# Sample attention of a streaming encoder layer in plain FP32 products, with earlier loads and later memory stores

## The chip, the cores and the metric

The kernel runs on one core of a Trainium2 chip. The core has a matrix engine (TensorE, PE; its weight loads are shown apart as PEld), VectorE (DVE), ScalarE (ACT), GpSimd (POOL) and SyncE (SP), whose queue issues nearly all DMA transfers of this kernel. Products land in PSUM, everything else lives in SBUF or in DRAM. The metric is the device time of one execution in microseconds (us); several executions are timed, and the median is compared.

## The reference

One layer of a hybrid encoder for two request groups that share the weights: a prompt of 1024 rows and a sample of 64 rows with cached keys and values. Per group: RMSNorm and a combined projection, chunk-band attention A (8 heads of 64), forgetting attention B (8 heads of 64), the output product w_o, a memory cross-attention and a convolutional FFN. The part that the change touches is the attention of the sample group; here it is, cut:

```python
def attend(q, k, v, bias, mask):
    scale = q.shape[-1] ** -0.5
    logits = jnp.einsum('bqhd,bkhd->bhqk', q, k).astype(jnp.float32) * scale
    ...
    p = jax.nn.softmax(logits, axis=-1)
    return jnp.einsum('bhqk,bkhd->bqhd', p.astype(v.dtype), v)

def chunk_band_attn_sample(qa, ka, va, cache_k, cache_v, table):   # A: 512 cached rows + 64
    k = jnp.concatenate([cache_k, ka], axis=1)
    v = jnp.concatenate([cache_v, va], axis=1)
    ...
    return attend(qa, k, v, bias, None).reshape(b, s, h * d)

def forget_attn_sample(qb, kb, vb, logf, cache_k, cache_v, cache_logf):   # B: 1024 cached rows + 64
    k = jnp.concatenate([cache_k, kb], axis=1)
    v = jnp.concatenate([cache_v, vb], axis=1)
    cum_h = jnp.cumsum(all_logf, axis=1).transpose(0, 2, 1)
    bias = cum_h[..., p:, None] - cum_h[..., None, :]
    ...
    return attend(qb, k, v, bias, mask).reshape(b, s, h * d)

def mem_kv(mem, g_mem, w_mkv, g_mk):
    kv = rms_norm(mem, g_mem) @ w_mkv
    k = rms_norm(kv[..., :D_MODEL].reshape(b, n, H_M, HEAD_DIM_M), g_mk)
    v = kv[..., D_MODEL:].reshape(b, n, H_M, HEAD_DIM_M)
```

The memory keys and values are outputs too, beside the new keys and values of both groups.

## The kernel before

**Split products.** Nearly every product of the kernel is made of two-part operands. An FP32 tensor x is split into hi, a copy of x in the type FP32R, and lo = x - hi, also FP32R; a product is then the sum of hi x hi, hi x lo and lo x hi (`SPLIT`), or of two of these where one side needs no second part. The split costs a cast on ACT and a subtraction on DVE or POOL per operand. Only transposes and a few products with a matrix of ones use plain FP32.

**Stages.** For each of eight head pairs (0 to 3 are A, 4 to 7 are B) the projection of the prompt, its norms and its attention run interleaved; the sample's rows of the same pair are projected in `proj_sample`, which stores their queries and keys to the DRAM tensor `sqk` and their values to `sv`. After the last pair the pool of projection weights is closed and a small pool `mp` is opened in its place. Now the memory projection runs: 16 units (8 blocks of 256 columns by 2 row tiles), each in four pieces of six products (`mem_piece`, L637), 65 entries in the list `line`. `mem_end` (L703) normalises and stores the finished block, `mem_turn` (L733) transposes a key block and stores it. The first 23 entries run beside the last four steps of the prompt's attention (`LEFT`), the other 42 beside the sample pairs (`PER`), in the order B, B, B, B, A, A, A, A (`SAMPLES`). A weight block of the memory projection is loaded in two halves by `load_wm` (L621) up to two units ahead and split by `split_wm` (L629, L630) one unit ahead.

**A sample pair.** `load` (L752) fetches the pair's queries and keys (sqd), new values (svn), the bias (s, one of four buffers in the pool wk), two cached key tiles of 128 partitions (kraw; the keys of one head stand in the array twice, one copy below the other) and the value chunks (vraw). `prep` (L775) splits the new values, transposes queries and keys on TensorE and splits them with the gains in `gained` (L276, L277). `splitk` (L796) and `splitv` (L806) split cached keys and values. `score` (L814) makes, per head, the products of q with hi and lo keys, adds the bias and takes the row minimum on DVE (L828, L830), and runs the exponential on ACT (L836). `turn` (L840) transposes the probabilities on TensorE and splits them (L851, L852), `sum` (L855) multiplies them with both parts of the values (L863) and joins the parts (L870, L871), `out` (L873) transposes the result.

**Order.** The loop over x runs `score` of pair x, turns and sums of pair x - 1 and `prep` and the key splits of pair x + 1, woven into the pieces of the memory projection; `load` of pair x + 1 is called at the start of step x. The first pair is loaded and prepared after the pool of the local attention (`wa`) is closed, since its tiles live in the pool `mq` that takes its place. The framework assigns buffers and writes each engine's instructions in an order of its own from priorities, dependences and modelled readiness, so an instruction may stand before others that precede it in the code; on each engine and on SP's queue the order is then fixed, and an instruction that waits holds those behind it. In the step in which the line of pieces has run out, `open_left` (L986) closes the left pools, opens those of the w_o product, and issues the loads of the mixes (after the last pair's last load, `issue_after`) and of w_o.

Of the kernel before, what the change touches and what calls it, by code (L numbers as in the profile page):

```python
# [41 lines left out]
def hybrid_step(ctx: ExitStack, tc: tile.TileContext, i: dict, o: dict):  # L42
# [658 lines left out]
    kvs, stores = {}, []  # L701

    def mem_end(n, t):  # L703
        pj = mpj.pop((n, t))[:, :256]
        if n == 7:
            kv = wk.tile([P, 256], F32, name="sq", bufs=2)
        else:
            kv = mp.tile([P, 256], F32, name="kv", bufs=2)
# [3 lines left out]
        if n < 4:  # L712
# [7 lines left out]
            nc.sync.dma_start(o["mk"][rows_, cols], kv)  # L720
        else:
# [6 lines left out]
            if n == 7:  # L728
                stores.append(store)
            else:  # L730
                store()

    def mem_turn(n, t):  # L733
        kv = kvs.pop((n, t))
        if n < 4:
            tq = bank("PT").rearrange("p (a b) -> p a b", a=4)
            for c in range(2):
                pe.transpose(tq[:, c], kv[:, c * P:(c + 1) * P], ident)
            kt = mp.tile([P, 2, P], F32, name="kt", bufs=2)
            dve.tensor_copy(kt, tq[:, 0:2])  # L740
            nc.sync.dma_start(kmd[n].rearrange("d p t -> p d t")[:, :, t * P:(t + 1) * P], kt)

    class Sample:
# [8 lines left out]
        def load(self):  # L752
            p, n = self.p, self.ctx + S
            self.qd = mq.tile([S, 4, P], F32, name="sqd", bufs=2)
            nc.sync.dma_start(self.qd.rearrange("t h d -> t (h d)"), sqk[p])
            self.vraw = mq.tile([S, 2, 64], F32, name="svn", bufs=2)
            nc.sync.dma_start(self.vraw.rearrange("t h d -> t (h d)"), sv[p])
# [7 lines left out]
            self.kraw, self.craw, self.kc, self.vc = [], [], {}, []  # L765
            for h in range(2):
                raw = mq.tile([P, T], F32, name="kraw", bufs=3)[:, :self.ctx]
                nc.sync.dma_start(raw, self.ck[2 * (p % 4) + h])
                self.kraw.append(raw)
            for c in range(self.nc):  # L770
                raw = mq.tile([P, 4, 2, 64], F32, name="vraw", bufs=3)
                self.loaded = nc.sync.dma_start(raw.rearrange("p k h d -> p (k h d)"), self.cv[p % 4, c])
                self.craw.append(raw)

        def prep(self):  # L775
            p = self.p
            self.vn = mq.tile([S, 2, 2, 64], F32R, name="svh", bufs=2)
            dve.tensor_copy(self.vn[:, :, 0], self.vraw)
            pool.tensor_tensor(self.vn[:, :, 1], self.vraw, f32(self.vn[:, :, 0]), op=ALU.subtract)
            tq = bank("tq").rearrange("p (a b) -> p a b", a=4)  # L780
            for x in range(4):
                pe.transpose(tq[:, x, :S], self.qd[:, x], ident[:S, :S])
            self.z = zq[SAMPLES.index(p) % 2]
            self.q = self.z[:, 0:4:3]
            self.kn = [mq.tile([P, 2, S], F32R, name=f"skn{x}", bufs=2) for x in range(2)]
            gained((self.q, self.z[64:, 0:4:3], tq[:, 0:2, :S], gd[:, p // 4, 0:1], LOWER),
                   (self.kn[0], self.kn[1], tq[:, 2:4, :S], gd[:, p // 4, 1:2], ALL))
# [8 lines left out]
        def splitk(self, h):  # L796
            k = self.kraw.pop(0)
            for c in range(self.nc):
                raw = k[:, c * 512:(c + 1) * 512]
                hi = mq.tile([P, 512], F32R, name="kchi", bufs=4)  # L800
                lo = mq.tile([P, 512], F32R, name="kclo", bufs=4)
                act.copy(hi, raw)
                dve.tensor_tensor(lo, raw, f32(hi), op=ALU.subtract)
                self.kc[h, c] = hi, lo

        def splitv(self):  # L806
            for c in range(self.nc):
                raw = self.craw.pop(0)
                v = mq.tile([P, 4, 2, 2, 64], F32R, name="vc", bufs=3)
                act.copy(v[:, :, :, 0], raw)  # L810
                pool.tensor_tensor(v[:, :, :, 1], raw, f32(v[:, :, :, 0]), op=ALU.subtract)
                self.vc.append(v)

        def score(self):  # L814
# [5 lines left out]
            for h in range(2):  # L820
                q = self.z[:, 2 * h:2 * h + 2].rearrange("p h t -> p (h t)")
                for m in range(2):
                    first, last = h + m == 0, h + m == 2
                    for c in range(self.nc):
                        pe.matmul(sp[:, c], q, self.kc[h, c][m], start=first, stop=last)
                    pe.matmul(sn[:, 0, :S], q, self.kn[m][:, h], start=first, stop=last)
# [13 lines left out]
        def turn(self, c):  # L840
# [6 lines left out]
            hi = wk.tile([P, 4, 2, P], F32R, name="pth", bufs=2)[:, :, c % 2]  # L847
            lo = wk.tile([P, 4, 2, P], F32R, name="ptl", bufs=2)[:, :, c % 2]
            for x in range(n):
                pe.transpose(pt[:rows_, x], self.s[:, (4 * c + x) * P:(4 * c + x) * P + rows_], ident)  # L850
            act.copy(hi[:rows_, :n], pt[:rows_, :n])  # L851
            dve.tensor_tensor(lo[:rows_, :n], pt[:rows_, :n], f32(hi[:rows_, :n]), op=ALU.subtract)  # L852
            self.pt[c] = hi, lo

        def sum(self, c):  # L855
            last = c == self.nc
            if c == 0:
                self.op = ps.tile([P, 2, P], F32, name="O", bufs=1).rearrange("p a b -> p (a b)")
# [1071 lines left out]
```

## Time and profile before

| what | value |
|---|---|
| median of 3 runs | 1782.7 us (1782.04 to 1783.35) |
| profiled execution | 1783.02 us |
| its span, from the first to the last instruction | 1781.2 us |
| outside the span | 1.8 us |
| mean granted TensorE clock | 0.991 |
| DMA over the span | 112 GB/s mean |

Each profile is of one execution. The engine row gives busy time, its share of the span and the number of instructions. The row of slices cuts the span into 40 equal parts and shows the busy share of each in tenths. A group of instructions has its line, engine, operation, output and inputs by the program's names, shapes, count, busy time, mean duration in ns of one, and the idle time of its engine just before, with what ended it. TensorE overlaps its instructions, so the distance of two starts in the timeline, not the duration of one, is what an instruction costs there.

### The profile page before, as it was taken

Reading aid. Unit: us, or ns where it says so; the run is one execution under the profiler, and the core shown is the slowest. Engines: PE = TensorE matmul, PEld = TensorE weight load, DVE = VectorE, ACT = ScalarE, POOL = GpSimd, SP = SyncE. Lnnn points to the kernel's source line nnn. Section 1 sums busy time; section 2 is a strip of 40 time slices with the busy share of each in tenths; the row PEclk is TensorE's granted clock in tenths of the full one; section 3 lists DMA queues with packets and bytes.
Section 4 is the critical chain, followed back from the end, with each engine's and each line's share of the span. In section 5 each row is a group of like instructions: output and inputs, shape, how many; then the busy total and the mean of one; then the engine's idle time right before and its main releaser. Section 6 shows DMA issues by size and latency. Waiting matters only on the chain.

```text
span 1781.2 us, 34032 instructions
## 1 busy us (share of the span) xinstructions
PE 1714.3 (96%) x12432; PEld 1666.1 (94%) x12432; DVE 1216.3 (68%) x2659; ACT 942.3 (53%) x2074; POOL 644.8 (36%) x931
## 2 busy tenths in 40 slices
PE   7898999999999888999999999999999999999998
PEld 6788999999998877999999999999999999999998
DVE  5767667677677777433444379877777777649986
ACT  6755667677677666434555456343333333434442
POOL 3656666878778443453433612100000000000000
PEclk8999999999999998999999999999999999999999
DMA  7322122122132666641111563222222222793332
GB/s 248 98 65 66 57 73 80 47 75 79 47 113 88 190 223 213 188 139 45 55 53 54 161 212 103 74 79 73 91 82 88 76 73 73 237 339 125 116 104 87
DMA packets 136697, 199.88 MB, mean 112 GB/s; under 512 B 21240, under 2 KB 77688, under 8 KB 136528
## 3 DMA queue, kind: packets, MB, share of 16 engines
q1 hardware_dynamic: 136528, 197.70, 35.4%
q8 instruction: 98, 1.61, 0.4%
q14 instruction: 71, 0.58, 0.1%
HBM read 155.35 MB, written 45.44 MB: 113 GB/s over the span
## 4 chain that ended last, share of the span: by engine, by line
PE 51%; DVE 1%; POOL 1%; issue 1%; ACT 0%; DVEq 0%; POOLq 0%; ACTq 0%
PE W L1485 25%; PE W L1809 13%; PE pj L958 7%; PE W L958 2%; PE S L1228 1%; PE tq L1264 1%; PE O L1264 1%; POOL lo L940 1%; PE PT L1251 0%; PE O L1228 0%; PE PT L1209 0%; POOL s L1243 0%; DVE f L1350 0%; ACT hi L939 0%; DVE qhi L1337 0%
## 5 line engine op out<-in xcount | busy, mean ns | idle before, releaser
L310 PE MATMUL pj<-whi,xhi 128*128 128x384 f32 (+1 forms) x512 | 194.5, 380 | 2.9 <-ACT xhi L138 1.7
L310 PE MATMUL pj<-wlo,xhi 128*128 128x384 f32 (+1 forms) x512 | 175.8, 343 | 4.6 <-POOL wlo L131 4.6
L310 PE MATMUL pj<-whi,xlo 128*128 128x384 f32 (+1 forms) x512 | 174.5, 341 | 0.0
L1591 POOL COPY s<-gp 128x2 f32<-128x2 f32 x22 | 15.8, 719 | 334.6 <-DVE gp L1590 334.6
L1485 PE MATMUL W<-h,hi 128*128 128x272 f32 x704 | 134.4, 288 | 1.4 <-ACT qlo L1621 1.4
L515 ACT ACTIVATE s<-s,mx 128x640 f32<-128x640 f32 (+7 forms) x128 | 94.4, 738 | 75.9 <-DVE mx L513 75.1
L1809 PE MATMUL W<-f,hi 128*128 128x272 f32 x672 | 127.1, 287 | 0.0
L552 DVE TENSOR_TENSOR ptl<-PT,pth 128x512 fp32r<-128x512 f32 (+2 forms) x192 | 99.6, 522 | 35.2 <-ACT pth L551 33.4
L1485 PEld LDWEIGHTS W<-h,hi 128*128 128x128 f32 x704 | 110.8, 188 | 1.7 <-ACT qlo L1621 1.6
L551 ACT CAST pth<-PT 128x512 fp32r<-128x512 f32 (+2 forms) x192 | 84.8, 448 | 39.3 <-PE PT L550 37.6
L1809 PEld LDWEIGHTS W<-f,hi 128*128 128x128 f32 x672 | 105.3, 188 | 0.1
L310 PEld LDWEIGHTS pj<-wlo,xhi 128*128 128x128 f32 x512 | 98.9, 193 | 6.1 <-POOL wlo L131 6.1
L310 PEld LDWEIGHTS pj<-whi,xhi 128*128 128x128 f32 x512 | 98.6, 193 | 4.6 <-ACT xhi L138 2.2
L1485 PE MATMUL W<-h,lo 128*128 128x272 f32 x352 | 101.8, 289 | 0.0
L310 PEld LDWEIGHTS pj<-whi,xlo 128*128 128x128 f32 x512 | 97.2, 190 | 0.5 <-DVE xlo L139 0.4
L1809 PE MATMUL W<-f,lo 128*128 128x272 f32 x336 | 96.7, 288 | 0.0
L550 PE MATMUL PT<-ident,s 128*128 128x128 f32 x528 | 89.3, 275 | 5.3 <-DVE ptl L552 5.1
L958 PE MATMUL pj<-a,hi 128*128 128x384 f32 (+1 forms) x352 | 90.5, 339 | 3.9 <-ACT hi L939 3.1
L1349 ACT CAST hi<-raw 128x512 fp32r<-128x512 f32 x68 | 42.2, 621 | 98.2 <-PE W L1485 58.3
L510 PE MATMUL S<-kh,q 128*128 128x256 f32 (+1 forms) x304 | 76.2, 277 | 15.9 <-DVE mx L513 15.7
L518 POOL TENSOR_SCALAR s<-s,ssum 128x640 f32<-128x640 f32 (+6 forms) x96 | 70.4, 734 | 41.4 <-DVE ssum L516 30.7
L550 PEld LDWEIGHTS PT<-ident,s 128*128 128x128 f32 x528 | 65.5, 140 | 14.9 <-DVE ptl L552 9.1
(552 smaller groups left out, 6060.7 us busy)
## 6 DMA issues: line engine op xcount, KB each, us to landing
raw<-in_w_down_dram SPq DMA_DIRECT2D x45, 256.0 KB, 2.8
wraw<-in_w_dram SPq DMA_DIRECT2D x56, 192.0 KB, 2.6
raw<-in_w_up_dram SPq DMA_DIRECT2D x41, 256.0 KB, 2.8
h<-ad SPq DMA_DIRECT2D x32, 272.0 KB, 5.3
mwraw<-in_w_mkv_dram SPq DMA_DIRECT2D x16, 512.0 KB, 4.8
raw<-in_w_mo_dram SPq DMA_DIRECT2D x32, 256.0 KB, 3.3
kvraw<-in_w_down_dram SPq DMA_DIRECT2D x32, 256.0 KB, 3.0
ad<-t SPq DMA_DIRECT2D x22, 272.0 KB, 2.2
```

Source lines behind the costliest of these rows:

```text
L310: pe.matmul(pj[:, :nw], x_part(a, k, t * P, P), wt[k][b][:, :nw], start=n == 0, stop=n == 3 * KT - 1)
L510: pe.matmul(sp[:, a:a + (k1 - k0) * P], q, kk[:, h, src], start=m == 0, stop=m == 1)
L515: act.activation(s[:, :n], s[:, :n], ACT.Exp, bias=mx, scale=-1.0, accum_out=sm)
L518: pool.tensor_scalar(s[:, :n], s[:, :n], sm, 1.0, op0=ALU.mult, op1=ALU.mult)
L550: pe.transpose(pt[:, b - ch[0]], self.s[j][:, (b - w0) * P:(b - w0 + 1) * P], ident)
L551: act.copy(hi[:, f:f + n, j], pt[:, f:f + n])
L552: dve.tensor_tensor(lo[:, f:f + n, j], pt[:, f:f + n], f32(hi[:, f:f + n, j]), op=ALU.subtract)
L958: pe.matmul(out()[:, :cn], w[a][:, k % 4], x[b][k][:, c0:c0 + cn], start=k == 0 and (a, b) == SPLIT[0], stop=k == KT - 1 and (a, b) == SPL ...
L1264: pe.matmul(op[:, a0:a1], v[x][:, b, d * P:(d + 1) * P], self.p2[y][:, b, a0:a1], start=n == 0, stop=n == 5)
L1349: act.copy(hi, t)
L1485: pe.matmul(w[:, z, :Q], a(p, j), rights[j][b][:, z * Q:z * Q + Q], start=fresh and begin and j == 0 and x == 0, stop=final and end and j ...
L1809: pe.matmul(ws[m][:, z, :Q], la[p][:, m * P:(m + 1) * P], ra[b][:, z * Q:z * Q + Q], start=first and y == 0 and what in opening, stop=fina ...
```

## The change

Three things are done together.

- **Plain FP32.** Queries, keys, probabilities and values of the sample attention are no longer split. The queries of both heads stand in one tile with zeros in the off-diagonal blocks, the keys of both heads are loaded into the two halves of one tile (64 partitions each, the first copy alone), and one plain FP32 product per 512 columns gives the scores of both heads. `splitk` and `splitv` are gone; `turn` copies the transposed probabilities once, on ACT or DVE in turn; `sum` makes one plain product per 128 rows, and reads the new values from svn as loaded. `prep` first copies the query pair and the key pair next to each other on POOL, and transposes two tiles instead of four.
- **Earlier loads.** `load` no longer fetches the bias (`load_bias` does). The four B pairs have their tiles in the pool `mp` (keys in three buffers, value chunks in six), the A pairs in `mq`. Pairs 0, 1 and 2 of the order are loaded, and pair 0 is prepared, beside the last local steps; in the loop, `load` is called three pairs ahead.
- **Later stores.** The memory's stores are put on a list and issued at piece 1 of the next unit; their tiles get a third buffer.

```diff
-    kvs, stores = {}, []
+    kvs, stores, waiting = {}, [], []
+
+    def flush(n):
+        while len(waiting) > n:
+            waiting.pop(0)()
...
-            kv = mp.tile([P, 256], F32, name="kv", bufs=2)
+            kv = mp.tile([P, 256], F32, name="kv", bufs=3)
...
-            nc.sync.dma_start(o["mk"][rows_, cols], kv)
+            waiting.append(lambda: nc.sync.dma_start(o["mk"][rows_, cols], kv))
...
-                store()
+                waiting.append(store)
...
-            kt = mp.tile([P, 2, P], F32, name="kt", bufs=2)
+            kt = mp.tile([P, 2, P], F32, name="kt", bufs=3)
             dve.tensor_copy(kt, tq[:, 0:2])
-            nc.sync.dma_start(kmd[n].rearrange("d p t -> p d t")[:, :, t * P:(t + 1) * P], kt)
+            waiting.append(lambda: nc.sync.dma_start(kmd[n].rearrange("d p t -> p d t")[:, :, t * P:(t + 1) * P], kt))
...
         def load(self):
+            p = self.p
+            self.early = SAMPLES.index(p) < 4
+            self.pl = mp if self.early else mq
+            self.qd = self.pl.tile([S, 4, P], F32, name="sqd", bufs=2)
+            nc.sync.dma_start(self.qd.rearrange("t h d -> t (h d)"), sqk[p])
+            self.vraw = self.pl.tile([S, 2, 64], F32, name="svn", bufs=2)
+            nc.sync.dma_start(self.vraw.rearrange("t h d -> t (h d)"), sv[p])
+            self.k = self.pl.tile([P, self.ctx], F32, name="kraw", bufs=3)
+            for h in range(2):
+                nc.sync.dma_start(self.k[h * S:h * S + S], self.ck[2 * (p % 4) + h, 0:S])
+            self.v = []
+            for c in range(self.nc):
+                raw = self.pl.tile([P, 4, 2, 64], F32, name="vraw", bufs=6 if self.early else 3)
+                self.loaded = nc.sync.dma_start(raw.rearrange("p k h d -> p (k h d)"), self.cv[p % 4, c])
+                self.v.append(raw)
+
+        def load_bias(self):
...
         def prep(self):
             p = self.p
-            self.vn = mq.tile([S, 2, 2, 64], F32R, name="svh", bufs=2)
-            dve.tensor_copy(self.vn[:, :, 0], self.vraw)
-            pool.tensor_tensor(self.vn[:, :, 1], self.vraw, f32(self.vn[:, :, 0]), op=ALU.subtract)
             tq = bank("tq").rearrange("p (a b) -> p a b", a=4)
-            for x in range(4):
-                pe.transpose(tq[:, x, :S], self.qd[:, x], ident[:S, :S])
...
+            heads = self.qd.rearrange("t (x h) (a d) -> t x h a d", x=2, a=2)
+            for x in range(2):
+                self.pair = self.pl.tile([S, 2, 64], F32, name="pair", bufs=2)
+                pool.tensor_copy(self.pair, heads[:, x, :, 0])
+                pe.transpose(tq[:, x, :S], self.pair.rearrange("t h d -> t (h d)"), ident[:S, :S])
+            self.z = zeroed[self.early][SAMPLES.index(p) % 2]
+            self.kn = self.pl.tile([P, S], F32, name="skn", bufs=2)
+            for h in range(2):
+                r = slice(h * S, h * S + S)
+                act.activation(self.z[r, h], tq[r, 0, :S], ACT.Copy, scale=gd[r, p // 4, 0:1])
+            dve.tensor_scalar(self.kn, tq[:, 1, :S], gd[:, p // 4, 1:2], None, op0=ALU.mult)
...
-        def splitk(self, h):
...
-        def splitv(self):
...
-            for h in range(2):
-                q = self.z[:, 2 * h:2 * h + 2].rearrange("p h t -> p (h t)")
-                for m in range(2):
-                    first, last = h + m == 0, h + m == 2
-                    for c in range(self.nc):
-                        pe.matmul(sp[:, c], q, self.kc[h, c][m], start=first, stop=last)
-                    pe.matmul(sn[:, 0, :S], q, self.kn[m][:, h], start=first, stop=last)
+            q = self.z.rearrange("p h t -> p (h t)")
+            for c in range(self.nc):
+                pe.matmul(sp[:, c], q, self.k[:, c * 512:(c + 1) * 512], start=True, stop=True)
+            pe.matmul(sn[:, 0, :S], q, self.kn, start=True, stop=True)
...
-            act.copy(hi[:rows_, :n], pt[:rows_, :n])
-            dve.tensor_tensor(lo[:rows_, :n], pt[:rows_, :n], f32(hi[:rows_, :n]), op=ALU.subtract)
-            self.pt[c] = hi, lo
+            if c % 2:
+                dve.tensor_copy(t[:rows_, :n], pt[:rows_, :n])
+            else:
+                act.copy(t[:rows_, :n], pt[:rows_, :n])
+            self.pt[c] = t
...
+            v = self.vraw.rearrange("p (o h) d -> p o h d", o=1) if last else self.v[c]
             for x in range(n):
-                for m in range(2):
-                    pe.matmul(self.op, self.pt[c][m][:rows_, x], v[:rows_, x].rearrange("p h a d -> p (h a d)"),
-                              start=c == 0 and x == 0 and m == 0, stop=last and m == 1)
+                pe.matmul(self.op, self.pt[c][:rows_, x], v[:rows_, x].rearrange("p h d -> p (h d)"),
+                          start=c == 0 and x == 0, stop=last)
             if last:
-                t = wk.tile([P, 64], F32, name="st", bufs=2)
...
-                    act.activation(t[r], self.op[r, h * P + 64:h * P + P], ACT.Copy, scale=self.r[r])
-                    dve.scalar_tensor_tensor(self.u[r], self.op[r, h * P:h * P + 64], self.r[r], t[r], op0=ALU.mult, op1=ALU.add)
+                    act.activation(self.u[r], self.op[r, h * S:h * S + S], ACT.Copy, scale=self.r[r])
...
                 mem_piece(n, t, c)
+                if c == 1:
+                    flush(0)
...
-    for n in LEFT:
-        step(n, substeps())
+    zeroed = {True: zeros(mp)}
+    samples = [Sample(p) for p in SAMPLES]
+    ahead = [[samples[0].load], [samples[1].load], [samples[0].load_bias, samples[2].load], [samples[0].prep]]
+    for n, f in zip(LEFT, ahead):
+        step(n, substeps() + f)
...
-    samples[0].load()
-    step(0, [samples[0].prep, lambda: samples[0].splitk(0), lambda: samples[0].splitk(1)])
...
         if nxt:
-            nxt.load()
+            nxt.load_bias()
+        if x + 3 < len(samples):
+            samples[x + 3].load()
...
-            new = [cur.score, cur.splitv]
+            new = [cur.score]
         if nxt:
-            fin = [nxt.prep, lambda: nxt.splitk(0), lambda: nxt.splitk(1)]
+            fin = [nxt.prep]
```

50 lines of the change are left out of this document (10 added, 40 removed).

## The prediction

> **What bounds the kernel now.** I read the page first, then busy time by stretch, then TensorE's waits and shapes in the stretch that the change touches. The page's span, engine row and PE's row of 40 slices (44.5 us each):
>
> ```profile
> span 1781.2 us, 34032 instructions
> PE 1714.3 (96%) x12432; PEld 1666.1 (94%) x12432; DVE 1216.3 (68%) x2659; ACT 942.3 (53%) x2074; POOL 644.8 (36%) x931
> PE   7898999999999888999999999999999999999998
> ```
>
> TensorE (PE) is the bound nearly everywhere; the visible holes after the start are slices 14 to 16, about 579 to 712 us. Busy time by stretch (columns: stretch, its length, busy us and instructions of PE, PEld, DVE, ACT, POOL, granted clock, DMA share, GB/s), first four stages, then three short stretches inside the third:
>
> ```profile
> 580.00:611.00 31.00, 26.73 (x218) 25.34 (x217) 23.02 (x54) 18.11 (x50) 14.11 (x17) 1.00 0.53 156
> 611.00:697.00 86.00, 76.84 (x498) 66.54 (x496) 60.19 (x142) 55.32 (x135) 34.23 (x35) 0.92 0.67 212
> 697.00:721.00 24.00, 19.76 (x98) 16.87 (x98) 17.89 (x45) 17.70 (x52) 6.75 (x5) 0.86 0.74 236
> 721.00:800.00 79.00, 79.00 (x480) 79.00 (x479) 31.31 (x52) 32.45 (x65) 39.77 (x34) 1.00 0.56 170
> ...
> 635.10:638.50 3.40, 3.40 (x14) 2.68 (x14) 2.21 (x5) 1.75 (x6) 0.47 (x1) 0.50 0.34 84
> 648.80:652.20 3.40, 3.40 (x12) 3.00 (x13) 3.25 (x5) 3.40 (x8) 1.84 (x2) 0.50 0.88 252
> 672.70:679.50 6.80, 6.19 (x25) 5.65 (x26) 3.30 (x10) 1.54 (x4) 2.14 (x3) 0.50 0.18 52
> ```
>
> 580 to 611 holds the last local steps; 611 to 697 the sample pairs beside 42 pieces of the memory projection; 697 to 721 the ramp into the w_o product; from 721 PE has no gap, so what is saved before it reaches the end in full. What PE waits for between 611 and 697 (total, times, longest):
>
> ```profile
> PE S L825 <- DVE kclo L803: 4.2, 4, 1.9
> PE pj L637 <- DVE kv L719: 1.6, 1, 1.6
> PE PT L875 <- DVE su L871: 1.2, 2, 0.9
> PE O L863 <- DVE ptl L852: 0.5, 2, 0.3
> PE tq L782 <- DMA svn<-sv: 0.4, 1, 0.4
> ```
>
> The largest is a split that the change takes away. How much of the 86 us is work? Groups by shape in the stretch (count, busy, mean ns, idle before), and starts in the timeline (start, duration), the latter since PE overlaps its instructions and a mean duration is no rate:
>
> ```profile
> L637 PE MATMUL pj<-mwhi,mhi 128*128 128x256 f32 x81 | 25.1, 310 | 1.6 <-DVE kv L719 1.6
> L863 PE MATMUL O<-vc,ptl 128*128 128x256 f32 x40 | 11.4, 309 | 0.5 <-DVE ptl L852 0.5
> L825 PE MATMUL S<-kclo,sq 128*128 128x512 f32 x22 | 10.9, 495 | 4.2 <-DVE kclo L803 4.2
> L850 PE MATMUL PT<-ident,s 128*128 128x128 f32 x41 | 7.6, 295 | 0.3 <-ACT smix L877 0.2
> L826 PE MATMUL tq<-skn,sq 128*128 128x64 f32 x28 | 4.3, 258 | 0.2 <-DVE skn L277 0.2
> L782 PE MATMUL tq<-ident,sqd 64*128 64x64 f32 x32 | 3.6, 232 | 0.4 <-DMA svn<-sv 0.4
> ...
> 620.56 0.39 PE L825 MATMUL S<-kclo,sq 128*128 128x512 f32 x1
> 620.79 0.28 PE L637 MATMUL pj<-mwhi,mlo 128*128 128x256 f32 x1
> 620.91 0.28 PE L637 MATMUL pj<-mwhi,mhi 128*128 128x256 f32 x1
> 695.10 0.40 PE L782 MATMUL tq<-ident,sqd 64*128 64x64 f32 x4
> 695.44 0.39 PE L637 MATMUL pj<-mwhi,mhi 128*128 128x256 f32 x1
> ```
>
> So a 512-column product costs 0.23 us, a 256-column one 0.12, a query/key transpose 0.085. The memory line is 3 x 81 x 0.12 = 29.2, the value sums 2 x 40 x 0.12 = 9.6 and some 12 on the new rows 1.4, the scores 2 x 22 x 0.23 = 10.1 and 28 x 0.12 = 3.4, transposes 32 x 0.085 = 2.7 and about 59 small ones at 0.11 (an estimate from these rows) 6.5: together 63 us. The other 23 us of the 86 are loss: 7.9 in the five waits, 6.8 by the clock (13.6 us at 0.50), and 8.3 in short hand-overs.
>
> **The change part by part.** Plain FP32 products first. The trace has some: the products with ones (L1396) take two instructions each, and so do those of two columns (L1134).
>
> ```profile
> L1396 PE MATMUL W<-sq,ones x4: 392/392/393, 1032.5 to 1033.2; 128*128 128x272 f32 x4
> 801.86 0.38 PE L1134 MATMUL PT<-ones,kSh 128*128 128x2 f32 x2 [0.20 <-POOL kSh L1119]
> 802.10 0.60 PE L958 MATMUL pj<-a,hi 128*128 128x384 f32 x2
> ```
>
> Four starts in 0.7 us are 0.23 us per pass of 272 columns; a pass of two columns still costs 0.12. By columns a pass of 512 costs 0.23 x 512/272 = 0.43. Scores: a pair of group B falls from 8 x 0.23 + 4 x 0.12 = 2.32 to 4 x 0.43 + 2 x 0.12 = 1.96, one of A from 1.40 to 1.10; eight pairs save 2.6 us. Value sums: 56 chunks of two split products become 56 of two passes over 128 columns, by columns 0.11, by the floor 0.12: nothing (at worst 0.23 a pass as at 272 columns, +12; at best -1). Prep loses 16 of 32 transposes: 1.4. PE work: **-4.0 us**.
>
> The engines beside it, 611 to 697, where the splits stood (same columns as above), and two waits of the DMA-issuing queue SP:
>
> ```profile
> L803 DVE TENSOR_TENSOR kclo<-kraw,kchi 128x512 fp32r<-128x512 f32 x22 | 18.8, 882 | 1.1 <-ACT kchi L802 0.9
> L852 DVE TENSOR_TENSOR ptl<-PT,pth 128x512 fp32r<-128x512 f32 x10 | 6.9, 688 | 2.4 <-ACT pth L851 2.4
> L802 ACT CAST kchi<-kraw 128x512 fp32r<-128x512 f32 x22 | 12.8, 618 | 0.2 <-DMA kraw<-in_cbk_dram 0.2
> L810 ACT CAST vc<-vraw 128x512 fp32r<-128x512 f32 x11 | 6.7, 618 | 1.5 <-PE O L863 1.1 <-DMA vraw<-in_cbv_dram 0.4
> L811 POOL TENSOR_TENSOR vc<-vraw,vc 128x512 fp32r<-128x512 f32 x11 | 15.6, 1422 | 28.6 <-ACT vc L810 18.6 <-DVE kclo L803 6.8 <-issue 3.0
> SPq L725 <- ACT kv L722: 16.8, 3, 6.7
> SPq L768 <- DVE kclo L803: 6.1, 3, 4.0
> ```
>
> DVE loses 18.8 and half of 6.9 (each probability chunk is now copied once, by ACT or by DVE in turn), so at least 22 of its 60 us; ACT 12.8 + 6.7 and about 3, so 22 of 55; POOL 15.6 of 34, and gains 16 small copies of query and key pairs. None of this is PE time by itself; it is worth the waits it ends. kclo, svn and half of su and ptl end: 4.2 + 0.4 + 0.6 + 0.25 = **-5.5**. kv (1.6) stays, as its chain of square, rsqrt and multiply stays. What is late next is the softmax (reduce, exp, reciprocal) of the pair before, with steps some 2 us shorter to hide it: **+2**, bounded by 0 and by the 4.2 that kclo had. Of the 8.3 in hand-overs, DVE and ACT emptied by two fifths should take about 40%: **-3.5** (0 to -8.3).
>
> The clock: it stood at 0.50 in the three stretches above, 6.8 us of work lost, in a stage whose waits are short and many; from 721 on, without waits, it stands at 1.00. With most named waits gone I take the longest of the three and a fifth of the other two as gone: 3.4 + 0.6 = **-4** (0 to -6.8).
>
> Moved: `load` of three B pairs goes into the last local steps, each with sqd, svn, two key halves and two value chunks on SP, past the stores of mixes and the w_mkv loads there; prep of the first pair too, with two POOL copies, two transposes, two ACT and one DVE instruction and the POOL mask, past the local softmax scaling. That work leaves 611 to 697 and enters 580 to 611, where PE has 31 - 26.7 = 4.3 us visibly idle: I count 0 (-3 to +3). Memory stores are queued one piece after their data is ready: the 16.8 us that SP stood behind kv is gone for the loads behind it; PE gains nothing by itself (0 to -1.6). Ramp 697 to 721: it starts when the last memory piece frees the left pool, then w_o loads and splits; kchi, vc and kclo of the last pair leave ACT and DVE there, but the pair covers less: **-1** (-4 to +2).
>
> Added waits: the fourth pair's `load` wants the key buffer of the first (three buffers, free after its scores) and its value buffers (free after its sums, a step later); svn is now read by the sums, with two buffers, so the third pair's svn waits as long. Behind them on SP stand w_mkv loads, stores and bias loads, and the splits of w_mkv on ACT, DVE and POOL wait for those.
>
> Sum: -4.0 - 5.5 + 2 - 3.5 - 4 + 0 - 1 = -16. The profiled execution took 1783.0 us (1.8 outside its span), 0.3 above the median of 1782.7: 1783.0 - 16 = **1767 us**.
>
> **The rivals.**
>
> *Only the PE work goes.* The hand-overs are PE's own order and the softmax chain, and where kclo was late the exp is late: -4, **1779**. For: su and ptl in the list of waits belong to the value side, not to the splits of keys. Against: kclo is the largest wait by far.
>
> *The stage becomes PE-bound,* as 721 to 800 is: all 23 us of loss and the 4 go: **1756**. Against: PE lost 4.3 of 31 us before 611 with none of these splits there.
>
> *The clock stays halved.* If waits of 1.9 us and less are not what halves it, the 4 us of the clock stay: -12, **1771**. For: the waits are short beside stretches of 3.4 us. Against: 721 to 800, without waits, has the full clock. The Trainium skill (TensorE: Matmul & The Clock Gate, Part 1) lets the clock fall only after an idle window of about 3.4 us, which speaks for this rival; the trace does not agree with it, since no named wait between 611 and 697 is above 1.9 us and the clock was halved three times.
>
> *SP blocks (slower).* A load placed ahead of its free buffer holds SP, and the w_mkv loads behind it. SP already stood 4.0 us for a key buffer. A blocked w_mkv load decides once its delay exceeds the step of lead it has (86 us over some seven steps, 12 us). For three such loads, each 5 us beyond that, PE stands 15 us and 5 more at half clock; with 15 of the 16 kept, **1788**. Against: the first pair's bias load was issued 22 us before the query load that precedes it in the code, so SP's order follows what is ready; and the key loads shrink.
>
> ```profile
> 589.45 1.11 SPq L764 DMA_DIRECT2D s<-negs  x2
> ...
> 611.64 0.45 SPq L755 DMA_DIRECT2D sqd<-sqk  x1
> ...
> kraw<-in_cbk_dram SPq DMA_DIRECT2D x8, 512.0 KB, 5.3
> s<-negs SPq DMA_DIRECT2D x8, 272.0 KB, 3.8
> ```
>
> A half of 256 KB now goes to 64 partitions, as negs does: 3.8 us in place of 5.3, not half. The Trainium skill (SBUF — State Buffer, "Can I just issue two DMAs to hit both halves?") says that two such halves serialize at half the ports, hence that nothing is saved; then this rival keeps its chance where the row would lower it.
>
> *The loads come no earlier* (their slots free late): svn's 0.4 stays, **1768**.
>
> **How the numbers follow.** Forecast 0.45 (1760 to 1775), clock stays 0.10 (1768 to 1775), PE work alone 0.18 (1775 to 1781), PE-bound 0.12, SP blocks 0.10, no earlier 0.05. The range 1755 to 1781 leaves out the slower case and the far ends. 0.2%, about what a measurement here can tell from no change, is 3.6 us: faster ends at 1779. Faster: 0.45 + 0.10 + 0.12 + 0.05 + 0.10 of the 0.18 = 0.82; same: the other 0.08 and a little of the blocked case, 0.09; slower 0.09.
>
> **What would show it.** Right: no kclo or vc group; 512-column passes 0.43 apart; DVE under 40 us where it had 60; the last memory piece some 13 to 16 us earlier; clock near 1.00 there. Wrong: sums 0.2 us apart; PE waiting for exp or w_mkv splits by several us; the stretch to the last memory piece unchanged.

## The result, and the profile after

The kernel with the change takes **1760.1 us** (median of four, 1758.7 to 1761.8) beside 1783.0 for the kernel before: a ratio of 0.987 (0.9853 to 0.9887), 22.9 us less. The forecast of 1767 had the sign and its range (1755 to 1781) holds the time, but 7 us of the gain were not in its sum. Its profiled execution took 1761.8 us.

The page of the kernel after: span, engine row, PE's row of 40 slices (44.0 us each now) and its granted clock.

```profile
span 1760.0 us, 33766 instructions
PE 1700.5 (97%) x12376; PEld 1652.9 (94%) x12376; DVE 1180.9 (67%) x2591; ACT 920.2 (52%) x2030; POOL 629.4 (36%) x933
...
PE   7898999999999999999999999999999999999999
PEclk9999999999999999999999999999999999999999
```

The span is 21.2 us shorter, PE's busy time only 13.8 (1714.3 - 1700.5). So about a third of the shorter span, 7.4 us, is time in which PE had stood idle. The holes of slices 14 to 16 are gone. Busy time by stretch (columns as in the prediction): the memory stage, the ramp into w_o, and the two stretches in which the clock was still halved.

```profile
613.00:680.00 67.00, 63.56 (x438) 55.58 (x437) 31.08 (x79) 34.16 (x91) 17.76 (x29) 0.95 0.64 190
680.00:699.00 19.00, 15.49 (x91) 13.37 (x91) 13.66 (x38) 16.10 (x47) 5.47 (x4) 1.00 0.91 295
...
643.90:647.30 3.40, 3.40 (x17) 3.40 (x18) 2.03 (x4) 1.29 (x2) 1.05 (x1) 0.50 1.05 297
657.50:660.90 3.40, 3.40 (x17) 3.40 (x18) 3.40 (x1) 2.03 (x5) 3.40 (x3) 0.50 0.04 15
```

The stretch that was 611 to 697 (86 us, PE busy 89% of it) is 613 to 680 (67 us, PE busy 95%). DVE falls from 60.2 to 31.1 us there, ACT from 55.3 to 34.2, POOL from 34.2 to 17.8. The ramp is 19 us instead of 24. What PE still waits for from 613 to 680 is a split of the memory's weights, not of a key:

```profile
PE pj L637 <- POOL mwlo L630: 2.3, 2, 1.6
PE PT L837 <- ACT smix L863: 0.7, 1, 0.7
PE tq L790 <- DVE smx L818: 0.4, 2, 0.3
```

The price of a plain FP32 product, from starts in the timeline of the kernel after (start, duration of the group, xcount): four passes of 512 columns, then what follows them; eight of 128 columns, then what follows.

```profile
637.71 1.88 PE L813 MATMUL S<-kraw,sq 128*128 128x512 f32 x4
639.43 0.33 PE L814 MATMUL tq<-skn,sq 128*128 128x64 f32 x2
...
676.62 1.05 PE L851 MATMUL O<-vraw,pth 128*128 128x128 f32 x8
677.42 0.36 PE L637 MATMUL pj<-mwhi,mhi 128*128 128x256 f32 x1
```

(639.43 - 637.71)/4 is 0.43 us a pass, (677.42 - 676.62)/8 is 0.10.

**Where the time went** is best read from the first and the last score product, since the eight pairs follow one another. Two views of single lines (count: shortest/median/longest in ns, first to last start). In the kernel before the first split of the keys starts the chain and the second ends it; after, there is one kind.

```profile
L825 PE MATMUL S<-kchi,sq x24: 387/438/792, 618.1 to 700.1; 128*128 128x512 f32 x24
L825 PE MATMUL S<-kclo,sq x24: 391/434/792, 618.9 to 700.6; 128*128 128x512 f32 x24
```

```profile
L813 PE MATMUL S<-kraw,sq x24: 590/592/697, 611.6 to 681.3; 128*128 128x512 f32 x24
```

The span is then three pieces: the **start** (first score), the **chain** (first to last score) and the **rest** (last score to the end). Before: 618.1 + 82.5 + 1080.6 = 1781.2. After: 611.6 + 69.7 + 1078.7 = 1760.0. So -6.5, -12.8 and -1.9. The memory projection, which the prediction followed, runs along with the chain: its first product starts at 571.1 before and 572.0 after, its last at 695.9 and 679.2.

### The profile page after: what moved, and what is told of

Its sections match the earlier page's. It is cut to its first block, busy times and chain, and to the rows that moved or that the text cites. A ratio compares the mean times of both kernels' runs of the same rounds, so it can differ in the third digit from the quotient of the medians.

```text
span 1760.0 us, 33766 instructions
## 1 busy us (share of the span) xinstructions
PE 1700.5 (97%) x12376; PEld 1652.9 (94%) x12376; DVE 1180.9 (67%) x2591; ACT 920.2 (52%) x2030; POOL 629.4 (36%) x933
## 4 chain that ended last, share of the span: by engine, by line
PE 46%; DVE 4%; issue 2%; ACT 1%; DMA 1%; POOL 1%; SPq 0%; DVEq 0%; ACTq 0%; POOLq 0%
PE W L1481 25%; PE W L1805 10%; PE pj L951 7%; PE S L1224 1%; PE tq L1260 1%; PE O L1260 1%; POOL lo L933 1%; DVE f L1346 1%; PE PT L1247 0%; DVE lo L1346 0%; ACT hi L1345 0%; DMA f<-x2d 0%; PE O L1224 0%; DMA x2d<-qhi 0%; DMA raw<-in_w_down_dram 0%
## 5 line engine op out<-in xcount | busy, mean ns | idle before, releaser
L515 ACT ACTIVATE s<-s,mx 128x640 f32<-128x640 f32 (+7 forms) x128 | 94.4, 738 | 75.4 <-DVE mx L513 74.7
L951 PE MATMUL pj<-a,hi 128*128 128x384 f32 (+1 forms) x352 | 86.9, 332 | 3.4 <-ACT hi L932 2.6
```

Source lines behind the costliest of these rows:

```text
L515: act.activation(s[:, :n], s[:, :n], ACT.Exp, bias=mx, scale=-1.0, accum_out=sm)
L951: pe.matmul(out()[:, :cn], w[a][:, k % 4], x[b][k][:, c0:c0 + cn], start=k == 0 and (a, b) == SPLIT[0], stop=k == KT - 1 and (a, b) == SPL ...
```

## The experiments

Medians are of four or five executions (ten of stores_alone, eight of early_alone), ratios (with 95% intervals) to the kernel before on the same chip. Starts, chains and rests come from one profiled execution each; the memory stage began anywhere from 568.8 to 573.8 in these although the code ahead of it hardly differs, so a start is good to some 2.5 us; where a start is compared below, the first memory product of that execution is given too. The kernels ran on several chips, and two of them are called different only where their ratios differ by more than the intervals leave open.

| kernel | median us | ratio to before | start | chain | rest |
|---|---|---|---|---|---|
| before | 1783.0 | 1 | 618.1 | 82.5 | 1080.6 |
| after | 1760.1 | 0.987 (0.9853 to 0.9887) | 611.6 | 69.7 | 1078.7 |
| fp32_alone | 1771.5 | 0.9941 (0.9923 to 0.996) | 622.0 | 71.2 | 1078.9 |
| stores_alone | 1779.1 | 0.9979 (0.9969 to 0.9989) | 618.9 | 77.5 | 1081.4 |
| early_alone | 1777.6 | 0.9967 (0.9954 to 0.998) | 613.6 | 84.4 | 1078.8 |
| fp32_early | 1760.1 | 0.9864 (0.9845 to 0.9882) | 609.2 | 69.2 | 1076.3 |
| dead_splits | 1765.6 | 0.9904 (0.9887 to 0.992) | 613.4 | 75.4 | 1077.1 |
| pair8 | 1758.1 | 0.9864 (0.9849 to 0.9879) | 612.4 | 66.3 | 1077.5 |
| fp32_roomy | 1771.1 | 0.9928 (0.991 to 0.9946) | 623.5 | 70.4 | 1078.1 |
| scores_twice | 1762.4 | 0.9878 (0.986 to 0.9895) | 611.3 | 72.6 | 1076.9 |
| first_early | 1765.0 | 0.9908 (0.9889 to 0.9927) | 611.9 | 70.7 | 1080.6 |
| three_ahead_late | 1771.3 | 0.9943 (0.9928 to 0.9958) | 621.7 | 72.0 | 1078.2 |
| left3 | 1760.1 | 0.9883 (0.9866 to 0.9899) | 605.3 | 74.5 | 1077.6 |
| left3_roomy_wo | 1752.8 | 0.984 (0.9826 to 0.9855) | 603.2 | 70.0 | 1077.2 |

### One part at a time

**Plain FP32 alone**: the kernel after with the loads one pair ahead, from `mq`, and the stores at once.

```diff
-            self.early = SAMPLES.index(p) < 4
+            self.early = False
...
-    ahead = [[samples[0].load], [samples[1].load], [samples[0].load_bias, samples[2].load], [samples[0].prep]]
-    for n, f in zip(LEFT, ahead):
-        step(n, substeps() + f)
+    for n in LEFT:
+        step(n, substeps())
...
+    samples[0].load()
+    step(0, [samples[0].prep])
...
-            nxt.load_bias()
-        if x + 3 < len(samples):
-            samples[x + 3].load()
+            nxt.load()
```

> The kernel before with the plain FP32 products alone; loads one pair ahead from the pool that follows the local attention, stores at once. If the splits on DVE, ACT and POOL were what held the stage, this has most of the 22.9 us: 1762 to 1766, with no kclo wait, and the first pair's loads still issued near 611 us. If the SP queue and the early loads carry a good part, it stays above 1770.

Measured: 1771.5, half of the whole gain. The line of its scores, then busy time of the end of its stage, and PE's waits from 685 to 712:

```profile
L814 PE MATMUL S<-kraw,sq x24: 590/592/1078, 622.0 to 693.2; 128*128 128x512 f32 x24
```

```profile
685.00:711.00 26.00, 20.82 (x89) 16.79 (x90) 13.97 (x36) 16.85 (x49) 5.36 (x4) 0.74 0.80 250
```

```profile
PE PT L838 <- ACT s L825: 3.5, 2, 1.9
PE PT L862 <- ACT su L858: 0.7, 1, 0.7
```

The chain is as short as in the kernel after (71.2 against 69.7), but starts at 622.0, ten microseconds later. Its last memory product starts at 683.7, so the last pair stands alone for 9 us: PE waits for the exp of the softmax (`s` on ACT, 3.5 us) and runs at a mean clock of 0.74. So part of what was saved ahead of the last memory product is given back behind it.

**Later stores alone**, on the kernel before: only the list, its `flush` and the third buffers of the diff.

> The kernel before with the later stores alone (and the third buffers). If the stores are off the critical path: 1781 to 1785, SP's waits for kv and kt gone. If stores that hold SP delay the loads behind them enough to matter: 1775 or less.

Measured: 1779.1, so 3.7 us less, all of it in the chain (82.5 to 77.5). **Early loads alone**, also on the kernel before, with split products kept and five key buffers; the preparation of the first pair stays where it was.

```diff
-    for n in LEFT:
-        step(n, substeps())
+    ahead = [[samples[0].load], [samples[1].load], [samples[0].load_bias, samples[2].load], []]
+    for n, f in zip(LEFT, ahead):
+        step(n, substeps() + f)
...
-            nxt.load()
+            nxt.load_bias()
+        if x + 3 < len(samples):
+            samples[x + 3].load()
```

> The kernel before, split products and stores at once, with the early loads alone (three pairs ahead; five key buffers for heads in each pool; the first pair is still prepared and split after the local attention). If the loads help by themselves, through SP and through mix loads that no longer stand behind the last pair's key load: 1771 to 1776, and the first w_o product sooner than 8.4 us after the last memory piece. If they only undo what plain FP32 alone gave back (14.9 us there): 1779 to 1784.

Measured: 1777.6, 5.4 less: an earlier start (613.6), no shorter chain. **FP32 and early loads, stores at once**: the kernel after without its list of stores.

> The changed kernel with stores at once (two buffers): plain FP32 and early loads together. Later stores alone were worth 3.7 us before the change. If SP has slack once loads are ahead, they are worth nothing here: 1759 to 1762. If they add up: 1763 to 1766.

Measured: 1760.1, the same as the kernel after. So the later stores are worth 3.7 us alone and nothing that shows beside the other two parts. That key loads with three pairs of lead no longer mind the stores fits this, but no run tests it by itself. The three parts alone add up to 11.3 + 3.7 + 5.4 = 20.4 of the 22.9; put onto plain FP32, the early loads are worth 11.4.

### What plain FP32 saves: work or occupancy

**The splits back as unread work**: the kernel after, and beside it the ACT, DVE and POOL splits of keys and values, into tiles that nothing reads.

```diff
+                act.copy(hi, raw)
+                dve.tensor_tensor(lo, raw, f32(hi), op=ALU.subtract)
...
-            new = [cur.score]
+            new = [cur.score, cur.splitv]
...
-            fin = [nxt.prep]
+            fin = [nxt.prep, lambda: nxt.splitk(0), lambda: nxt.splitk(1)]
```

> The changed kernel with the splits of keys and values of the sample pairs put back as work that nothing reads (48 casts and subtractions of 512 columns for keys, 12 casts and 12 POOL subtractions for values); TensorE does the same as after. If emptier DVE, ACT and POOL are the gain, at least 8 us of the 22.9 are lost: 1768 to 1778. If the gain is in TensorE's own work, in the DMA and in the loads, it stays within 3 us of 1760.

Measured: 1765.6, between what the two theories expected; the chain goes from 69.7 to 75.4. Busy time from 612 to 685, and PE's largest waits from 613 to 690:

```profile
612.00:685.00 73.00, 63.67 (x431) 54.39 (x430) 52.36 (x106) 53.00 (x127) 38.54 (x45) 0.95 0.60 179
```

```profile
PE pj L637 <- POOL mwlo L630: 3.3, 2, 1.7
PE tq L790 <- DVE rsq_a L79: 1.6, 1, 1.6
PE PT L742 <- DVE kv L723: 1.4, 1, 1.4
PE O L865 <- DVE ptl L853: 1.1, 1, 1.1
```

PE waits for no split of a key here, since none is read. It waits for other things that DVE and POOL make, each a little later, so the 5.5 us come as many small delays rather than one large wait. They are not from occupied engines alone: an unread split also holds the key tile that it reads, and SP stood for one, from 600 to 700:

```profile
SPq L766 <- DVE kclo L811: 3.7, 1, 3.7
```

The kernel after has no such wait. How the 5.5 us divide between busy engines and held tiles was not separated.

**PE work added**: each 512-column score product of the kernel after is made twice into the same place.

```diff
-            for c in range(self.nc):
+            for c in [c for c in range(self.nc) for _ in range(2)]:
```

> The changed kernel with each 512-column score product made twice into the same bank, 12 more products of two passes: 12 x 2 x 0.43 = 10.3 us of TensorE work and nothing else. If the stage is now bound by TensorE, 9 to 11 us longer: 1769 to 1771. If TensorE waits there for a chain of other engines, part is hidden: 1762 to 1767.

```profile
L813 PE MATMUL S<-kraw,sq x48: 590/592/697, 611.3 to 683.9; 128*128 128x512 f32 x48
```

That is the line of its scores, 48 passes where there were 24: 24 x 0.43 = 10.3 us of PE work more. The time is 1762.4, 2.2 us more, which the intervals cannot tell from nothing (0.986 to 0.9895 beside 0.9853 to 0.9887). Its busy time from 612 to 685:

```profile
612.00:685.00 73.00, 72.69 (x476) 58.74 (x475) 30.58 (x84) 38.11 (x101) 19.92 (x29) 1.00 0.69 203
```

PE is now busy all through and the clock never falls, where the kernel after had 6.8 us of it at 0.50. The other 8 us of work went into PE's idle time and into the clock. So with 95% busy this stage was not PE-bound: some 8 us fit in for nothing.

**More buffers for the query and key pair**, named by PE's waits in the kernel after: POOL made `mwlo` late behind its `pair` copies, which had two buffers.

```diff
-                self.pair = self.pl.tile([S, 2, 64], F32, name="pair", bufs=2)
+                self.pair = self.pl.tile([S, 2, 64], F32, name="pair", bufs=8)
```

> The changed kernel with eight buffers in place of two for the query and key pairs that POOL copies. After the change TensorE waits 2.3 us for POOL's splits of w_mkv, which stand on POOL behind a pair copy that waits 2.7 and 10.5 us for the transposes of the pair before, and the clock is halved for 6.8 us right there. If the buffers cause this: 1754 to 1757. If w_mkv is late for another reason (its load stands late on SP, at 637 us), no change: 1759 to 1761.

Measured: 1758.1, and its interval (0.9849 to 0.9879) overlaps that of the kernel after (0.9853 to 0.9887): no difference shown. The named wait is gone, but PE's waits from 569 to 690 now are:

```profile
PE PT L742 <- DVE kv L723: 3.5, 2, 2.3
PE tq L790 <- DVE smx L818: 2.9, 2, 2.6
```

These two lines were 1.2 and 0.4 us there, but 2.3 of the 3.5 us for `kv` fall ahead of 600, so in the stage itself the wait for `mwlo` (2.3 us) gave way to one for `smx` (2.9). Its chain of 66.3 us is the shortest of all, but its memory pieces take 107.7 us as they do in the kernel after (107.4).

### What the early loads are worth, and why

**More buffers instead of earlier loads**: fp32_alone with four buffers of svn, sqd and keys and six of values, so that loads wait less for tiles.

> Plain FP32 alone, with four buffers for svn, sqd and keys and six for value chunks in place of 2, 2, 3 and 3. Plain FP32 alone had its last pair's loads on SP behind waits for buffers that the sums now hold (8.8, 6.0 and 5.1 us), and 14.9 us from the last memory piece to the first w_o product. If the buffers did that: 1762 to 1767 and about 8 us there. If loading one pair ahead is what is late: 1770 to 1773 and 13 us or more.

Measured: 1771.1, the same as fp32_alone. More buffers by themselves do not bring back the 11 us that it is slower than the kernel after.

**Three pairs ahead, but no head start**: fp32_early with every sample tile in `mq`, which opens only when the local steps are over, so the first load can't go before. All eight pairs now share the buffers of one pool (six for value chunks, the other counts as they were).

```diff
-            self.pl = mp if self.early else mq
+            self.pl = mq
...
-    ahead = [[samples[0].load], [samples[1].load], [samples[0].load_bias, samples[2].load], [samples[0].prep]]
-    for n, f in zip(LEFT, ahead):
-        step(n, substeps() + f)
+    for n in LEFT:
+        step(n, substeps())
...
+    for f in (samples[0].load, samples[0].load_bias, samples[1].load, samples[2].load):
+        f()
+    step(0, [samples[0].prep])
```

> Plain FP32 and loads three pairs ahead, all in the pool that opens after the local attention, so that the first pair cannot be loaded sooner; stores at once. Beside plain FP32 with early loads (1760.1) it lacks the head start alone. If the chain's start sets the end: first scores near 620 us and 1768 to 1773. If the distance of the loads does: 1760 to 1764.

Measured: 1771.3, as fp32_alone. Two views of one line each: the scores of this kernel, then those of fp32_early.

```profile
L813 PE MATMUL S<-kraw,sq x24: 590/592/697, 621.7 to 693.7; 128*128 128x512 f32 x24
```

```profile
L813 PE MATMUL S<-kraw,sq x24: 590/592/697, 609.2 to 678.4; 128*128 128x512 f32 x24
```

Two chains of 72.0 and 69.2 us, 12.5 us apart, while both memory stages begin alike (569.8 and 569.7). That is about the difference of the medians, 1771.3 against 1760.1. But the head start is not all that sets the two kernels apart. With one pool, SP stands much longer for svn tiles (L763); from 600 to 700 this line's largest wait in total is 3.6 us in fp32_early, and here

```profile
SPq L763 <- PE O L851: 15.3, 4, 8.6
SPq L763 <- PE tq L790: 12.3, 1, 12.3
```

And in this execution the clock stood at 0.50 from 614.7 to 621.5, right ahead of the first score: 3.4 of the 12.5 us. So the run shows that loads three pairs ahead gain nothing here without the head start; that the head start is the whole of the 11.2 us it does not show.

In SP's timeline the first key load goes out at 574.00 in the kernel after and at 614.46 in fp32_alone, 7.5 us before its first score at 622.0:

```profile
574.00 1.23 SPq L766 DMA_DIRECT2D kraw<-in_cbk_dram  x2
```

```profile
614.46 1.28 SPq L767 DMA_DIRECT2D kraw<-in_cbk_dram  x2
```

**Only the first pair early**: fp32_alone with pair 0 loaded and prepared beside the local steps, and all others one pair ahead.

> Plain FP32 alone (1771.5), and only the first pair loaded and prepared beside the last local steps; the other seven one pair ahead, stores at once. If the sample pairs are a chain that sets the end, and the early loads only start it sooner (first scores at 611 in place of 622 us): 1759 to 1764. If loads three pairs ahead, and the mix loads that then stand earlier on SP, are what matters: 1768 to 1772.

```profile
L815 PE MATMUL S<-kraw,sq x24: 590/592/697, 611.9 to 682.6; 128*128 128x512 f32 x24
```

Measured: 1765.0, so 6.5 of the 11.4 us. The line of its scores stands beside that of the kernel after within 1.3 us, and its median is 4.9 us above. But its memory stage began 2.4 us sooner (first product at 569.6, after at 572.0). Counted from there, its first score comes after 42.3 us instead of 39.6, its chain is 1.0 longer and its rest 1.9: together 5.6 us, close to the 4.9 of the medians. PE also waits for the exp again, 2.3 us (L839 for `s`). So what the other early loads add is spread over the start, the chain and the rest.

### A version that beats both

**An earlier chain still**: five more pieces of the memory projection moved out of the last local step into the pairs' steps.

```diff
-LEFT = (4, 5, 6, 8)
-PER = (4, 6, 7, 8, 6, 5, 6, 0, 0)
+LEFT = (4, 5, 6, 3)
+PER = (6, 7, 8, 8, 7, 5, 6, 0, 0)
```

> The changed kernel with five of the memory's pieces moved from the last local step to the sample steps (LEFT 4, 5, 6, 3; PER 6, 7, 8, 8, 7, 5, 6). The first scores come some 3 us sooner. If the chain of pairs sets the end and has idle TensorE time to take five pieces of 0.72 us: 1756 to 1759. If the stage is full: 1760 to 1762.

Measured: 1760.1. The start is 6.3 us earlier (1.1 of it as the memory stage began at 570.9) and the chain 4.8 longer, with five pieces more between its pairs: nothing gained. **The same with room**: in addition four buffers of svn and keys in both pools, in `mq` four of sqd and values and eight of pair, and the first three pieces of w_o loaded into tiles of `mq`, which need not wait for the left pool.

```diff
-                raw = self.pl.tile([P, 4, P], F32, name="raw", bufs=3)
-                nc.sync.dma_start(raw, srcs[self.n + len(self.raws)])
+                n = self.n + len(self.raws)
+                raw = mq.tile([P, 4, P], F32, name="raw0", bufs=3) if n < 3 else self.pl.tile([P, 4, P], F32, name="raw", bufs=3)
+                nc.sync.dma_start(raw, srcs[n])
```

> The same shift, with four svn and key buffers (in the second pool also four of sqd and value chunks and eight of the copied pairs), and the first three w_o tiles loaded into the second pool, ahead of the closing of the left pools. TensorE waited 2.6 us for the first w_o split after the change; if the w_o load was late there, the first w_o product follows the last memory piece by 5 us or less, and 1752 to 1757. If the splits of the mixes set it, as the left pools must close first, no gain on the shift alone.

Measured: **1752.8**, a ratio of 0.984 (0.9826 to 0.9855), 7.3 us less than the kernel after. The line of its scores and its busy time from 612 to 685:

```profile
L813 PE MATMUL S<-kraw,sq x24: 590/592/697, 603.2 to 673.2; 128*128 128x512 f32 x24
```

```profile
612.00:685.00 73.00, 69.59 (x490) 59.83 (x489) 37.10 (x96) 45.19 (x123) 22.32 (x29) 1.00 0.77 232
```

The start is 8.4 us earlier than in the kernel after (3.2 of it as the memory stage began at 568.8 instead of 572.0), and the chain no longer (70.0). The clock stands at 1.00. Whether the buffers or the early w_o tiles keep the chain short was not separated.

## Why the prediction came out as it did

**The step that failed** is the one on the moved loads: "That work leaves 611 to 697 and enters 580 to 611, where PE has 31 - 26.7 = 4.3 us visibly idle: I count 0 (-3 to +3)". It weighed the moved work as PE time and left out when the chain of pairs may start. Measured, the early loads are worth 11.4 us on plain FP32 (fp32_alone against fp32_early), nearly four times the end of the bound, and 5.4 us on the kernel before. The head start of pair 0 by itself gives 6.5 us of it (first_early), and loads three pairs ahead without a head start give nothing (three_ahead_late, where SP is also held for svn). How the other 4.9 us divide between the earlier pairs 1 and 2 and the longer lead of the rest is open.

That the sum came within 7 us is partly luck. It had 16 us for plain FP32, which alone gave 11.3, and nothing for the early loads, which gave 11.4 on top: two errors of opposite sign.

**The PE work (-4.0).** The prices held: 0.43 us a pass of 512 columns as forecast, and 0.10 a pass of 128 where "by the floor 0.12" was counted. The premise, that PE work saved there reaches the end in full, is in doubt: in the kernel after, 10.3 us of work added cost 2.2, which is not clear of nothing (scores_twice). No run takes PE work away by itself. The rival in which the stage becomes PE-bound does not fit: PE is still idle for 3.4 of the 67 us and at half clock for 6.8, and the time is 4 us above its 1756.

**The ended waits (-5.5), hand-overs (-3.5) and softmax (+2).** The waits for kclo, svn and ptl are gone from the list, and DVE, with 31.1 us, is under the 40 named. The splits put back as unread work cost 5.5 us (dead_splits), as a sum of small delays and with key tiles held, more than the 3.5 counted for emptied engines. PE's wait for the softmax, forecast as what is late next, is only 0.4 us in the kernel after (the row minimum `smx`); for the exp it is 3.5 us in fp32_alone, where the last pair stands alone, and 2.3 in first_early. So the +2 names a wait that shows in the kernels whose loads go one pair ahead.

**The clock (-4).** From 611 to 697 before there were 13.6 us at 0.50 and after there are 6.8, so 3.4 us of work returned: the size is right, and the rival in which the clock stays halved is out for this kernel. What is left are two stretches of 3.4 us, the number and length that the forecast had kept, but behind other waits: both begin right after PE waited for `mwlo`, where before it had waited for kv, su and kclo.

**The ramp (-1).** The rest, from the last score to the end, is 1.9 us shorter. But the ramp of the prediction starts with the last memory piece, and from the start of the last memory product to the end it is 1781.2 - 696.1 = 1085.1 us before and 1760.0 - 679.4 = 1080.6 after: -4.5, outside its -4 to +2. In fp32_alone it is 1772.1 - 684.3 = 1087.8. So much of what the early loads gain arrives here: the last score comes 4.5 us after the last memory product before, 8.9 in fp32_alone and 1.9 after.

**Later stores (0).** Right in the whole (fp32_early takes the same time) and wrong alone: 3.7 us on the kernel before, beyond the bound of 1.6. And the wait that it called gone is not: SP stood 16.8 us behind kv before, and from 600 to 700 still 10.6 in the kernel after (L729, first line of the next view) and 10.7 in stores_alone.

**SP blocks (the slower rival).** The waits of the queue SP in the kernel after, 600 to 700:

```profile
SPq L729 <- ACT kv L726: 10.6, 2, 6.8
SPq L770 <- PE PT L837: 4.6, 1, 4.6
SPq L766 <- PE tq L814: 3.8, 2, 2.3
SPq L763 <- PE O L851: 3.4, 2, 3.0
```

The mechanism is there as it was described: SP stands for value, key and svn tiles (L770, L766, L763) that scores and sums still hold, 11.8 us in all. But none of these waits passes 4.6 us, well inside the lead of 12 us from which it was to decide, so the price of 15 us and more never came due. A key half of 256 KB took 4.2 us to land (median of the B pairs), where 3.8 was counted and twice the size had taken 5.3. Four svn and key buffers on fp32_alone gained nothing either.

**The signs named ahead**: no group of kclo or vc, passes 0.43 apart, DVE under 40 us and a last memory piece 16.7 us earlier (13 to 16 were named) all came true, DVE in a stage that is 19 us shorter; the clock came to 0.95, not quite 1.00. Of the signs of error one appeared in part, PE waiting for a w_mkv split: 2.3 us.

## What to carry to other kernels

Where steps follow one another beside filler work, read the first and the last product of that chain: span = start + chain + rest says at once whether an edit moved the start or shortened the steps, which a sum of busy time can't say. Take the start from where the filler work begins, which moves by itself from one execution to the next. A load moved earlier is to be priced by what it lets start, not by the engine time that moves with it. Before a saving of work is counted as time, add that work twice: in this stage 95% busy hid some 8 us of slack.

## What the hardware showed unasked

**One DVE subtraction waited out four of POOL's.** In the kernel after, the subtraction that makes `mwlo` (two inputs in SBUF, 512 columns) took 0.67 us at its shortest and 5.85 at its longest. The line's DVE view, then DVE's and POOL's timelines at that place:

```profile
L630 DVE TENSOR_TENSOR mwlo<-mwraw,mwhi x16: 674/687/5853, 547.8 to 663.1; 128x512 fp32r<-128x512 f32 x16
```

```profile
655.05 6.55 DVE L630 TENSOR_TENSOR mwlo<-mwraw,mwhi 128x512 fp32r<-128x512 f32 x2
661.53 0.15 DVE L826 RECIPROCAL ssum<-ssum 128x1 f32<-128x1 f32 x1
```

```profile
656.08 4.97 POOL L630 TENSOR_TENSOR mwlo<-mwraw,mwhi 128x512 fp32r<-128x512 f32 x4
```

DVE's second subtraction ends at 661.6 (655.05 + 6.55) and so began at about 655.75. POOL runs four of the same kind from 656.1 to 661.1, and DVE ends 0.5 us after the last. The Trainium skill (SBUF — State Buffer, "Who interferes with whom") says that a DVE instruction with two SBUF inputs contends with a GpSimd instruction that reads SBUF, for a pair of ports that only one of the two can hold at a time. The trace agrees and shows more: four in a row held DVE off. The longest such subtraction was 1.8 us in the kernel before and 1.4 in fp32_alone, but 5.7 in fp32_early and in left3. It also happened on a smaller scale at 641.6, where DVE's two took 3.88 us beside two of POOL's; the row minimum of a pair stood behind them on DVE until 645.43, and the exp on ACT that needs it waited 3.5 us. What this costs at the end was not measured by itself.

**The clock fell without a long wait.** The two halved stretches of the kernel after begin at 643.9 and 657.5, each right behind a wait of PE for `mwlo`:

```profile
643.76 0.52 PE L637 MATMUL pj<-mwlo,mhi 128*128 128x256 f32 x1 [1.62 <-POOL mwlo L630]
657.39 0.50 PE L637 MATMUL pj<-mwlo,mhi 128*128 128x256 f32 x1 [0.70 <-POOL mwlo L630]
```

The waits are short, but they follow others: in the 3.4 us before the two stretches PE was busy 1.50 and 2.02 us. In scores_twice, with PE busy 72.69 of 73 us, the clock stays at 1.00. So no single long wait is needed. Low busy time is not enough either: from 682.8 to 686.2 PE was busy 0.85 of 3.4 us, and the clock stood at 1.00 there and up to 692. What decides is not shown.

**A plain FP32 product is two instructions** (24 in the trace for the 12 score products in the code), of 0.43 us each on 512 columns and 0.10 on 128, beside 0.23 and 0.12 for one product of split parts on 512 and 256 columns. So each of the two takes about twice as long per column. At 128 columns the time is still what the width gives (a quarter of 0.43), though a pass of two columns took no less (0.12).
